# Hybrid decoder mixer on one Trainium2 core: projections in quarter chunks, and half of the conv group moved from beside the sample attention to beside the prompt attention

## The chip, the cores and the metric

One core of one Trainium2 chip runs the whole program as one launch. The metric is device time in microseconds (us). All tensors come and go as float32. An engine takes its own instructions in order from its own queue: TensorE (PE), VectorE (DVE), ScalarE (ACT), GpSimd (POOL) and SyncE (SP, which issues most DMAs). Every order named below is an order within one such queue.

## What is computed

One decoder layer on 1024 prompt rows and 32 sample rows (8 requests of 4 tokens): an FFN, the mixer, a second FFN, a final norm. Only the mixer is touched:

```python
p = rms_norm(x) @ w_in           # columns: q | k | v | forget logits | B gate | C gate | conv input
uc = cg * u                      # conv group: C gate times conv input
# head group A: 8 heads of 64, forgetting attention
s = q.k/8 + sum of log f between key and query      # causal
o_prompt = softmax(s) @ v                            # 1024 x 1024, blocks of 128 queries
o_sample = softmax over 2048 paged cache rows and 4 new rows, per request
# head group B: 512 channels, short conv of width 3 over time
y = conv_w[0]*uc[t-2] + conv_w[1]*uc[t-1] + conv_w[2]*uc[t];   conv_out = bg * y
x = x + concat(rms_norm(o), rms_norm(conv_out)) @ w_out
```

The cache of keys and the cache of values are each read once through a page table: 8 requests x 16 pages of 128 rows x 512 float32, 33.6 MB each.

## The kernel before, in words

**A projection** has 128 columns of w_in. `K.weight` (L91) loads them, 0.524 MB, in one DMA issued by SP (L75, three buffers), and splits each half into a float32r head `wh` (ACT, L86) and rest `wl` (DVE, L88). The 1056 rows of the normed x lie in SBUF as `XH` and `XL`. `win` (L612) makes one *window*: 352 rows, 8 row blocks of D, three matmuls each (L103 to L105, `wh` by `XH`, `wh` by `XL`, `wl` by `XH`), so 24 matmuls into one bank `pg`. A projection is three windows. q, k and v are four projections each, the conv group is four tiles of three projections (C gate, conv input, B gate) and nine windows a tile. A conv tile also reads its 8 KB state and writes an 8 KB state (`out_cso`, L929), in its own small pieces.

**The sample attention** (`sample(g)`, L813, g = two groups of four requests) is a generator. Its cache comes in 64 *chunks* of four pages (`fetch`, L772: two pages issued by SP after a page number is read, two gathered by POOL; four buffers, fetched up to four ahead), 1.05 MB each. Order: 16 key chunks of group 0, 16 value chunks of group 0, 16 key chunks of group 1, 16 value chunks of group 1. A key chunk is 16 short matmuls into `sc` (L832), a value chunk 16 calls into `pv` (L874), all with 32-wide column tiles. The values of a group also need the new values, so `sample(0)` waits for `vnew` (all v projections).

**The driver** (L972 to L982) walks through the k projections, the v projections and the four conv tiles, window by window, and after each window takes 1.2, 0.9 or 1.5 steps of the sample generator (`RK`, `RV`, `RC`); what remains runs at the end.

**The prompt attention** (L1112 to L1128) follows and has the PE to itself: 8 heads x 8 query blocks of 128. Per block: `logits` (L1041, matmuls with `KA`/`KB` into `S`, a mask), softmax on ACT and DVE, `flip` (L1062: transposes of P in groups of up to four into a bank `ptp`, two banks, copied out by ACT), and every second block `weigh` (L1077: P times V for two query blocks into `O`, two banks). Even heads hold P and V as float32r heads and rests and use two matmuls of 128 x 128 by up to 256 columns (L1089, L1090); the rest of P costs a DVE subtraction (L1075). Odd heads (`NATIVE`) keep float32 and use 64-wide weights (L1085), which run as two passes. Logits run three blocks ahead, `weigh` four behind. The norm of the conv output (`conv_norm`, L999) is put in after blocks 28 and 60. `load_qk` (L1026) loads a head's operands one head ahead; behind that of head 6 the loads of w_out are allowed to start (`K.after`).

A framework scheduler places the instructions of these generators on each engine's queue with the waits that the data and buffers need; the queues below are what it made.

Of the kernel before, what the change touches and what calls it, by code (L numbers as in the profile page):

```python
# [39 lines left out]
NATIVE = (1, 3, 5, 7)  # L40
LA, PVD, PTB, PRB = 3, 4, 3, 4
CONV_AT = (28, 60)
RK, RV, RC = 1.2, 0.9, 1.5
# [384 lines left out]
def kernel(ctx: ExitStack, tc: tile.TileContext, io: dict):  # L428
# [141 lines left out]
    with ExitStack() as es:  # L570
# [41 lines left out]
        def win(ws, c, m=P):  # L612
            ps = pg.tile([P, 512], F32, tag="pg", name="pg")[:m, :MC]
# [7 lines left out]
        def proj(i, kind, t):  # L621

            ws = K.weight(io["w_in"][i], D)
            for c in range(NMC):
                ps = win(ws, c)
# [130 lines left out]
        forget(lambda: next(qs[0]))  # L756
# [31 lines left out]
        new = []  # L788
# [24 lines left out]
        def sample(g):  # L813
# [25 lines left out]
            pn = ptr.tile([P, 512], F32, tag="tr", name="pn")[:, :NS]  # L839
            QN = smp.tile([P, NHP, 32], F32, tag="QN", bufs=1, name="QN")  # L840
# [10 lines left out]
            if g == 0:  # L851
                load_gates(1)
            yield
            PT = smp.tile([P, PAGES + 1, P], F32, tag="PT", bufs=1, name="PT")
# [8 lines left out]
            yield  # L863
            while not new:
                yield
# [17 lines left out]
            nc.scalar.activation(M, pv, AF.Copy, scale=sm)  # L883
# [19 lines left out]
        def conv():  # L903
            for t in range(4):
# [8 lines left out]
                for c in range(NMC):  # L913
                    ps = win(ws, c)
                    g_ = mix.tile([P, MC], F32, tag="cg", bufs=3, name="cg")
                    nc.scalar.copy(g_, ps)
                    cg.append(g_)
                    yield
                ws = K.weight(io["w_in"][20 + t], D)
                for c in range(NMC):  # L920
                    ps = win(ws, c)
# [24 lines left out]
                for c in range(NMC):  # L946
                    ps = win(ws, c)
# [5 lines left out]
        def values():  # L953
            for t in range(NHP):
                ws = K.weight(io["w_in"][8 + t], D)
                for c in range(NMC):
                    ps = win(ws, c)
# [25 lines left out]
    es_x.close()  # L983
# [5 lines left out]
    opc = pool(es_r, "op_c")  # L989
    xo = [None] * NCH  # L990
    with ExitStack() as es:
        ap_ = pool(es, "ap", "left")
        ptr = pool(es, "ptr2", space=PSUM)
# [16 lines left out]
        def load_v(hp):  # L1010
            vt = ap_.tile([P, SEQ], F32, tag="vt", bufs=1, name="vt")
            nc.sync.dma_start(vt, v_d[hp])
            V = ap_.tile([P, 8, 2, HD], F32R, tag="V", bufs=2, name="V")
            VF = ap_.tile([P, 8, HD], F32, tag="VF", bufs=2, name="VF")
            for j0 in range(0, 8, 4):
                pt_ = ptr.tile([P, 512], F32, tag="tr", bufs=2, name="ptv")
# [3 lines left out]
                pv_ = pt_.rearrange("p (j a d) -> p j a d", j=4, a=2)  # L1020
                nc.scalar.copy(V[:, j0:j0 + 4, 0, :], pv_[:, :, 0, :])
                nc.vector.tensor_sub(V[:, j0:j0 + 4, 1, :], pv_[:, :, 0, :], V[:, j0:j0 + 4, 0, :])
                nc.scalar.copy(VF[:, j0:j0 + 4, :], pv_[:, :, 1, :])
            return V, VF

        def load_qk(h):  # L1026
# [5 lines left out]
            for dst, src in ((KA[:HD], kh[pr, :]), (KA[HD:], kh[pr, :]),  # L1032
# [3 lines left out]
                ins = nc.sync.dma_start(dst.bitcast(F32), src)  # L1036
            if h == 6:
                K.after = ins.ins
# [23 lines left out]
        def flip(h, i, Pr, pt2):  # L1062

            c0 = P * (i % 2)
            for j0 in range(0, i + 1, 4):
                n = min(4, i + 1 - j0)
                pt_ = ptr.tile([P, 512], F32, tag="tr", bufs=2, name="ptp")
# [3 lines left out]
                pv_ = pt_[:, :n * P].rearrange("p (j q) -> p j q", q=P)  # L1071
                hi = pt2[0][:, j0:j0 + n, c0:c0 + P]
                nc.scalar.copy(hi, pv_)
                if h not in NATIVE:
                    nc.vector.tensor_sub(pt2[1][:, j0:j0 + n, c0:c0 + P], pv_, hi)  # L1075

        def weigh(h, m, pt2):  # L1077
            V, VF = vs[h // 2]
            pr = slice(HD * (h % 2), HD * (h % 2) + HD)
            O = ppv.tile([P, 512], F32, tag="pv", bufs=2, name="O")  # L1080
            nj = 2 * m + 2
            for j in range(nj):
                c0 = P if j == nj - 1 else 0
                if h in NATIVE:
                    nc.tensor.matmul(O[:HD, c0:256], VF[:, j, :], pt2[0][:, j, c0:], start=j == 0,  # L1085
                                     stop=j == nj - 1)
                else:
                    w = V[:, j].rearrange("p c d -> p (c d)")
                    nc.tensor.matmul(O[:, c0:256], w, pt2[0][:, j, c0:], start=j == 0, stop=False)  # L1089
                    nc.tensor.matmul(O[:, c0:256], w, pt2[1][:, j, c0:], start=False, stop=j == nj - 1)  # L1090
            at = ap_.tile([P, 256], F32, tag="at", bufs=3, name="at")
            if h in NATIVE:
                nc.scalar.copy(at[pr], O[:HD, :256])
            else:
                nc.scalar.copy(at[pr], O[HD:, :256])
                nc.vector.tensor_add(at[pr], O[:HD, :256], at[pr])
            nc.sync.dma_start(at_d[h // 2][pr, 256 * m:256 * m + 256], at[pr])
# [237 lines left out]
```

## Time and profile before

| | us |
|---|---|
| three runs | 2160.84, 2164.36, 2169.01 (median 2164.36) |
| profiled execution | 2163.56, span 2161.8 |
| FFN 1, norm, q projections, forget gate | 0 to 819.5 |
| k, v, conv projections beside the sample attention | 819.5 to 1143.5 |
| prompt attention | 1143.5 to 1308.4 |
| w_out and FFN 2 | 1308.4 to 2161.8 |

The stages are cut where the PE's lines change. 1.76 us of the time lie around the span. In the timeline, PE instructions overlap: the time that one costs is the distance to the start of the next, not its printed length.

### The profile page before, as it was taken

The numbers are of one execution on the slowest core, as the hardware profiler recorded it, in microseconds if no ns is written. First come the engines' busy times: TensorE is split into PE (matmuls) and PEld (weight loads), VectorE is DVE, ScalarE is ACT, GpSimd is POOL, SyncE is SP. The second block draws the span as 40 slices with busy tenths as digits, with TensorE's granted clock in tenths as the row PEclk, the third lists the DMA queues.
The fourth block names the chain that finished last, engine by engine and source line by source line (L and its number), as shares of the span: only waits on it lengthen the run. The fifth ranks groups of instructions, "written<-read, shape, count | busy, mean of one in ns | idle before, by whom it ended". The sixth has DMA issues, their size and how long they took to land. (4 is left out here: it accounts for less than half of the span.)

```text
span 2161.8 us, 42854 instructions
## 1 busy us (share of the span) xinstructions
PE 2098.5 (97%) x16738; PEld 1995.7 (92%) x16738; DVE 1352.4 (63%) x2604; ACT 876.1 (41%) x1754; POOL 264.3 (12%) x367
## 2 busy tenths in 40 slices
PE   7999999999999989999898999999999999999998
PEld 7999999999999877897697777999999999999997
DVE  8877777776656742322226785897677677775354
ACT  6533333344434422211115774453333333454343
POOL 0010001110000054234340000001010101100000
PEclk9999999999999989999998999999999999999999
DMA  6222222247546549869886436432222222496353
GB/s 212 77 93 91 84 85 93 93 162 238 198 139 212 167 150 329 297 201 312 253 262 142 111 95 201 144 107 88 76 80 73 86 85 84 142 311 210 108 180 131
DMA packets 138795, 335.15 MB, mean 155 GB/s; under 512 B 28144, under 2 KB 47568, under 8 KB 137056
## 3 DMA queue, kind: packets, MB, share of 16 engines
q1 hardware_dynamic: 116736, 263.66, 38.6%
q0 software_dynamic: 21856, 68.76, 9.1%
q8 instruction: 131, 2.15, 0.4%
q14 instruction: 72, 0.59, 0.1%
HBM read 276.09 MB, written 56.24 MB: 154 GB/s over the span
## 5 line engine op out<-in xcount | busy, mean ns | idle before, releaser
L103 PE MATMUL ps<-op,wh 128*128 128x264 f32 x2604 | 742.2, 285 | 2.9 <-ACT op L192 2.4
L105 PE MATMUL ps<-op,wl 128*128 128x264 f32 x2604 | 744.4, 286 | 0.0
L104 PE MATMUL ps<-op,wh 128*128 128x264 f32 x2604 | 743.1, 286 | 0.0
L86 ACT CAST wh<-wraw 128x512 fp32r<-128x512 f32 x536 | 312.8, 600 | 487.6 <-PE ps L104 281.3
L88 DVE TENSOR_TENSOR wl<-wraw,wh 128x512 fp32r<-128x512 f32 x536 | 347.3, 663 | 250.1 <-ACT wh L86 238.7
L103 PEld LDWEIGHTS ps<-op,wh 128*128 128x128 f32 x2604 | 492.8, 189 | 4.4 <-ACT op L192 2.8
L104 PEld LDWEIGHTS ps<-op,wh 128*128 128x128 f32 x2604 | 491.4, 189 | 0.4 <-DVE op L193 0.2
L105 PEld LDWEIGHTS ps<-op,wl 128*128 128x128 f32 x2604 | 491.5, 189 | 0.2
L103 PE MATMUL ps<-h,wh 128*128 128x264 f32 x1408 | 402.0, 285 | 0.0
L104 PE MATMUL ps<-h,wh 128*128 128x264 f32 x1408 | 400.5, 284 | 0.0
L105 PE MATMUL ps<-h,wl 128*128 128x264 f32 x1408 | 398.1, 283 | 0.5 <-DVE wl L88 0.5
L105 PEld LDWEIGHTS ps<-h,wl 128*128 128x128 f32 x1408 | 264.9, 188 | 0.7 <-DVE wl L88 0.7
L104 PEld LDWEIGHTS ps<-h,wh 128*128 128x128 f32 x1408 | 264.8, 188 | 0.2
L103 PEld LDWEIGHTS ps<-h,wh 128*128 128x128 f32 x1408 | 264.8, 188 | 0.2
L103 PE MATMUL pg<-XH,wh 128*128 128x352 f32 x576 | 196.0, 340 | 8.2 <-DVE zl L631 4.2
L104 PE MATMUL pg<-XL,wh 128*128 128x352 f32 x576 | 190.5, 331 | 0.0
L105 PE MATMUL pg<-XH,wl 128*128 128x352 f32 x576 | 189.7, 329 | 0.0
L86 ACT CAST wh<-s 128x512 fp32r<-128x512 f32 x176 | 107.7, 616 | 115.7 <-PE ps L104 106.9
L103 PEld LDWEIGHTS pg<-XH,wh 128*128 128x128 f32 x576 | 111.6, 194 | 34.7 <-issue 11.9
L88 DVE TENSOR_TENSOR wl<-s,wh 128x512 fp32r<-128x512 f32 x176 | 120.7, 690 | 26.6 <-ACT wh L86 22.5
L326 POOL DMA_DIRECT2D h_d<-t x79 | 42.7, 540 | 598.3 <-DVE t L325 598.3
L104 PEld LDWEIGHTS pg<-XL,wh 128*128 128x128 f32 x576 | 111.8, 194 | 0.0
(274 smaller groups left out, 2610.5 us busy)
## 6 DMA issues: line engine op xcount, KB each, us to landing
wraw<-in_w2a SPq DMA_DIRECT2D x48, 512.0 KB
wraw<-in_w2b SPq DMA_DIRECT2D x48, 512.0 KB
h_d<-t POOLq DMA_DIRECT2D x176, 132.0 KB, 2.0
h<-h_d SPq DMA_DIRECT2D x88, 264.0 KB
kvraw<-in_kc SPq DMA_DIRECT2D x64, 256.0 KB
kvraw<-in_vc SPq DMA_DIRECT2D x64, 256.0 KB
wraw<-in_w1a SPq DMA_DIRECT2D x28, 512.0 KB
wraw<-in_w3a SPq DMA_DIRECT2D x28, 512.0 KB
```

Source lines behind the costliest of these rows:

```text
L86: nc.scalar.copy(wh, x)
L88: nc.vector.tensor_sub(wl, x, wh)
L103: nc.tensor.matmul(ps, w[0], x[0], start=start, stop=False)
L104: nc.tensor.matmul(ps, w[0], x[1], start=False, stop=False)
L105: nc.tensor.matmul(ps, w[1], x[0], start=False, stop=stop)
L326: nc.gpsimd.dma_start(h_d[2 * p + 1][:, f, :], t)
```

## The change

- `win` becomes a generator that yields after every 6 of its 24 matmuls (a quarter). The rates become 0.34, 0.34 and 0.45 sample steps a quarter (1.36, 1.36, 1.8 a window).
- `sample(g)` is cut in `sample_keys(g)` and `sample_values(g)`; the cache is walked as keys 0, keys 1, values 0, values 1, so two `PT` (transposed probabilities) exist at once.
- `conv` takes a list of tiles: 0 and 1 stay beside the sample attention, 2 and 3 (18 windows) run beside the prompt attention, at 2.6 steps of the `prompt` generator a quarter. For this `XH`, `XL`, the buffers `mixb` and two `pg` banks live on; `ptp`/`ptv` and `O` go from two banks to one each.
- P times V: all heads keep float32 and one `V`. The two query blocks of a pair go to the two 64-row halves of `O` by 64-wide column tiles, alternating; 128 columns each, two passes each. The float32r rests, their subtractions and `NATIVE` go.
- `weigh` two blocks behind (was four), five P buffers (was three); both `conv_norm` after the last conv tile, among the last blocks; `K.after` is gone.

The core of the diff:

```diff
-RK, RV, RC = 1.2, 0.9, 1.5
+RK, RV, RC = 0.34, 0.34, 0.45
+CONV_A = 2
+RP = 2.6
...
-            K.dot(ps, ws, [(XH[:, k, cs], XL[:, k, cs]) for k in range(KD)])
+            for k in range(0, KD, 2):
+                K.dot(ps, ws[k:k + 2], [(XH[:, i, cs], XL[:, i, cs]) for i in (k, k + 1)], k == 0, k == KD - 2)
+                if k < KD - 2:
+                    yield
             return ps
...
         for g in range(2):
             chunks += [(io["kc"], 4 * g + b, j) for j in range(4) for b in range(4)]
+        for g in range(2):
             chunks += [(io["vc"], 4 * g + b, j) for b in range(4) for j in range(4)]
...
-        A = chain(sample(0), sample(1))
+        A = chain(sample_keys(0), sample_keys(1), sample_values(0), sample_values(1))
         due = 0.0
-        for work, rate in ((chain(*(proj(NHP + t, "k", t) for t in range(NHP))), RK),
-                           (values(), RV), (conv(), RC)):
+        for work, rate in ((k_proj(), RK), (values(), RV), (conv(range(CONV_A)), RC)):
...
+        mix = pool(es, "mixb", "left")
+        pg = es.enter_context(tc.tile_pool(name="pgb", bufs=2, space=PSUM, reuse_waits="tile"))
...
-                pt_ = ptr.tile([P, 512], F32, tag="tr", bufs=2, name="ptp")
+                pt_ = ptr.tile([P, 512], F32, tag="tr", bufs=1, name="ptp")
...
+            O = ppv.tile([P, 512], F32, tag="pv", bufs=1, name="O")[:, :P]
+            halves = [slice(0, HD), slice(HD, P)]
+            for j in range(2 * m + 2):
+                for b, (pr, pt) in enumerate(zip(halves, pt2)):
+                    n = 2 * m + b
+                    if j <= n:
+                        nc.tensor.matmul(O[pr], V[:, j, vc], pt[:, j, :], start=j == 0, stop=j == n)
+                if j == 3 and m > 1:
+                    yield
...
+        A = prompt()
+        due = 0.0
+        for _ in conv(range(CONV_A, 4)):
+            due += RP
+            while due >= 1:
+                next(A, None)
+                due -= 1
```

POOL's queue from the forget-gate gathers (`R`) to the last cache gather, as a difference; one gather is one page, `in_kc` keys, `in_vc` values:

```order
 L599 DMA R<-in_lf,idl 128x128 x5
+L599 DMA kvraw<-in_kc,idx 128x512 x32
+L825 MEMSET S 128x96
 L599 DMA kvraw<-in_kc,idx 128x512 x24
-L599 DMA kvraw<-in_vc,idx 128x512 x8
-L818 MEMSET S 128x96
-L599 DMA kvraw<-in_vc,idx 128x512 x24
-L599 DMA kvraw<-in_kc,idx 128x512 x32
-L599 DMA kvraw<-in_vc,idx 128x512 x32
```

The alternation of keys and values by groups is gone: all 64 key gathers come first, and the 64 value gathers follow as one run.

PE's queue at the last value chunks of the sample attention; before:

```order
L105 MATMUL pg<-XH,wl 128x352
L874 MATMUL pv<-kvraw,PT 32x128 x32
L879 MATMUL pv<-VS,PT 32x128 x4
L103 MATMUL pg<-XH,wh 128x352
L104 MATMUL pg<-XL,wh 128x352
L105 MATMUL pg<-XH,wl 128x352
```

and after:

```order
L105 MATMUL pg<-XH,wl 128x352
L887 MATMUL pv<-kvraw,PT 32x128 x32
L892 MATMUL pv<-VS,PT 32x128 x4
L887 MATMUL pv<-kvraw,PT 32x128 x64
L892 MATMUL pv<-VS,PT 32x128 x4
L103 MATMUL pg<-XH,wh 128x352
L104 MATMUL pg<-XL,wh 128x352
L105 MATMUL pg<-XH,wl 128x352
```

Before, a whole window of projection follows the last chunks; now six chunks stand in a row, without a projection between them.

PE's queue in the middle of the prompt attention, at an even head; before:

```order
L1089 MATMUL O<-PTh,V 128x256
L1090 MATMUL O<-PTl,V 128x256
L1049 MATMUL S<-KA,QA 128x512
L1050 MATMUL S<-KB,QB 128x512
L1069 MATMUL ptp<-cst,Pr 128x128 x4
L1052 LDWEIGHTS idb
L1052 MATMUL S<-diag,idb 128x128
L1049 MATMUL S<-KA,QA 128x512
L1050 MATMUL S<-KB,QB 128x512
```

and after, where the conv tiles 2 and 3 run:

```order
L1079 MATMUL ptp<-cst,Pr 128x128 x4
L103 MATMUL pg<-XH,wh 128x352
L104 MATMUL pg<-XL,wh 128x352
L105 MATMUL pg<-XH,wl 128x352
L103 MATMUL pg<-XH,wh 128x352
L104 MATMUL pg<-XL,wh 128x352
L1079 MATMUL ptp<-cst,Pr 128x128
L105 MATMUL pg<-XH,wl 128x352
L1060 MATMUL S<-KA,QA 128x128
L1061 MATMUL S<-KB,QB 128x128
```

Projection matmuls now stand between one group of transposes and the next, and between transposes and logits.

## Rows read from the trace of the kernel before

**Rows 1.** Page, part 1: busy us, share of span, instructions.

```profile
PE 2098.5 (97%) x16738; PEld 1995.7 (92%) x16738; DVE 1352.4 (63%) x2604; ACT 876.1 (41%) x1754; POOL 264.3 (12%) x367
```

**Rows 2.** Windows by stage: stretch, length, then the columns named.

```profile
core 0: us, PE busy (x) PEld busy (x) DVE busy (x) ACT busy (x) POOL busy (x), PEclk, DMA share, GB/s
...
819.50:889.60 70.10, 67.91 (x421) 51.82 (x421) 16.16 (x31) 18.24 (x40) 29.92 (x32) 0.98 1.00 348
889.60:938.60 49.00, 48.84 (x317) 46.44 (x316) 14.22 (x22) 14.41 (x27) 3.30 (x4) 1.00 0.56 196
938.60:1006.00 67.40, 64.67 (x825) 58.62 (x828) 12.55 (x26) 10.12 (x19) 30.28 (x32) 0.97 0.85 284
1006.00:1071.00 65.00, 56.99 (x360) 42.58 (x356) 14.69 (x33) 6.93 (x13) 28.75 (x30) 0.92 0.91 274
1071.00:1143.50 72.50, 72.50 (x893) 67.29 (x886) 19.92 (x41) 13.72 (x25) 26.93 (x29) 1.00 0.79 233
1143.50:1165.00 21.50, 16.24 (x71) 12.94 (x70) 11.22 (x32) 7.69 (x23) 3.20 (x6) 0.68 0.67 163
1165.00:1308.40 143.40, 139.65 (x866) 103.40 (x864) 114.17 (x254) 108.99 (x265) 0.00 (x0) 1.00 0.42 101
```

**Rows 3.** Timeline of PE, 828.9 to 834.5: start, length, line, operation, count.

```profile
828.96 0.32 PE L104 MATMUL pg<-XL,wh 128*128 128x352 f32 x1
829.12 0.32 PE L105 MATMUL pg<-XH,wl 128*128 128x352 f32 x1
829.37 1.07 PE L832 MATMUL sc<-kvraw,QZ 128*32 128x512 f32 x8
830.37 0.43 PE L103 MATMUL pg<-XH,wh 128*128 128x352 f32 x1
...
834.43 0.64 PE L832 MATMUL sc<-kvraw,QZ 128*32 128x512 f32 x4
```

**Rows 4.** Windows: the fastest long stretch, and one behind a state write.

```profile
840.00:900.00 60.00, 60.00 (x395) 47.49 (x388) 18.04 (x30) 13.91 (x29) 25.61 (x26) 1.00 1.01 366
1025.00:1032.00 7.00, 7.00 (x48) 5.34 (x48) 0.98 (x3) 0.00 (x0) 3.21 (x5) 1.00 0.84 43
```

**Rows 5.** DMA view, 1022 to 1034: packets, and one of its issues.

```profile
DMA packets 1898, 1.82 MB, mean 152 GB/s; under 512 B 1295, under 2 KB 1295, under 8 KB 1897
...
out_cso<-E SPq DMA_DIRECT2D x1, 8.0 KB
```

**Rows 6.** Timeline of PE, 1036 to 1052: a key chunk that waits.

```profile
1046.90 1.93 PE L832 MATMUL sc<-kvraw,QZ 128*32 128x512 f32 x8 [8.01 <-DMA kvraw<-in_kc]
```

**Rows 7.** Timeline of PE, 1097.6 to 1100: a value chunk.

```profile
1097.92 1.08 PE L874 MATMUL pv<-kvraw,PT 128*32 128x128 f32 x32
```

**Rows 8.** Timeline of PE, 1150 to 1160: the first transposes of V.

```profile
1156.76 1.97 PE L1018 MATMUL ptv<-cst,vt 128*128 128x128 f32 x8 [2.12 <-DMA vt<-v_d]
```

**Rows 9.** Timeline of PE, 1301.8 to 1308.6: last P times V, odd head.

```profile
1301.94 6.48 PE L1085 MATMUL O<-PTh,VF 128*64 128x256 f32 x32
```

**Rows 10.** Groups by form in 1301.8 to 1308.6: the shapes of these 32.

```profile
L1085 PE MATMUL O<-PTh,VF 128*64 128x256 f32 x26 | 6.2, 381 | 0.0
L1085 PE MATMUL O<-PTh,VF 128*64 128x128 f32 x6 | 1.1, 272 | 0.0
```

**Rows 11.** Groups by form, PE, 1143.5 to 1310: all odd heads.

```profile
L1085 PE MATMUL O<-PTh,VF 128*64 128x256 f32 x128 | 33.6, 389 | 0.3 <-ACT rs L169 0.3
...
L1085 PE MATMUL O<-PTh,VF 128*64 128x128 f32 x32 | 6.4, 282 | 0.0
```

**Rows 12.** Timeline of PE, 1255.9 to 1256.5: even heads.

```profile
1256.11 0.28 PE L1090 MATMUL O<-PTl,V 128*128 128x256 f32 x1
1256.23 0.28 PE L1089 MATMUL O<-PTh,V 128*128 128x256 f32 x1
```

**Rows 13.** Timeline of all engines, 1299.8 to 1302.9: transposes, then their copies.

```profile
1300.91 1.09 PE L1069 MATMUL ptp<-cst,Pr 128*128 128x128 f32 x8
1301.61 1.07 ACT L1073 COPY PTh<-ptp 128x512 f32<-128x512 f32 x2 [0.38 <-PE ptp L1069]
```

More of the change, by code (lines that the diff above doesn't have):

```diff
@@ L624, in proj @@
             for c in range(NMC):
-                ps = win(ws, c)
+                ps = yield from win(ws, c)
                 cs, n = cols(c)
@@ L755 @@
         qs = [proj(t, "q", t) for t in range(NHP)]
-        forget(lambda: next(qs[0]))
+        forget(lambda: [next(qs[0]) for _ in range(4)])
         for g in qs:
@@ L787 @@
         taken = []
-        new = []
+        keys, new = [], []
         def kv_chunk():
@@ L839, in sample @@
             pn = ptr.tile([P, 512], F32, tag="tr", name="pn")[:, :NS]
+            if g == 0:
+                load_gates(1)
+            while not keys:
+                yield
             QN = smp.tile([P, NHP, 32], F32, tag="QN", bufs=1, name="QN")
@@ L901, in vnew, with conv @@
             new.append(VS)
-        def conv():
-            for t in range(4):
+        def conv(ts):
+            for t in ts:
                 q = nc.gpsimd if t == 3 else nc.sync
@@ L913, in conv @@
                 for c in range(NMC):
-                    ps = win(ws, c)
+                    ps = yield from win(ws, c)
                     g_ = mix.tile([P, MC], F32, tag="cg", bufs=3, name="cg")
@@ L920, in conv @@
                 for c in range(NMC):
-                    ps = win(ws, c)
+                    ps = yield from win(ws, c)
                     cs, n = cols(c)
@@ L946, in conv @@
                 for c in range(NMC):
-                    ps = win(ws, c)
+                    ps = yield from win(ws, c)
                     st = mix.tile([P, MC], F32, tag="st", bufs=3, name="st")
@@ L956, in values @@
                 for c in range(NMC):
-                    ps = win(ws, c)
+                    ps = yield from win(ws, c)
                     cs, n = cols(c)
@@ L970, in chain, with k_proj @@
                 yield from g_
[L972 removed]
+        def k_proj():
+            for t in range(NHP):
+                yield from proj(NHP + t, "k", t)
+            keys.append(True)
+        A = chain(sample_keys(0), sample_keys(1), sample_values(0), sample_values(1))
         due = 0.0
[L974 to L975 removed]
+        for work, rate in ((k_proj(), RK), (values(), RV), (conv(range(CONV_A)), RC)):
             for _ in work:
@@ L982 @@
             pass
-    es_x.close()
     for t in range(NHP):
@@ L1099 @@
         qk, vs, prs, pts = {}, {}, {}, {}
-        blocks = [(h, 2 * m + j) for h in range(H) for m in range(4) for j in range(2)]
-        qk[0] = load_qk(0)
+        blocks = [(h, i) for h in range(H) for i in range(8)]
         def ahead(n):
@@ L1126, with behind, prompt @@
-        for k in range(len(blocks) - PVD, len(blocks)):
-            if k % 2:
-                weigh(blocks[k][0], blocks[k][1] // 2, pts.pop((blocks[k][0], blocks[k][1] // 2)))
+        def behind(k):
+            if k >= 0 and k % 2:
+                h, i = blocks[k]
+                yield from weigh(h, i // 2, [pts.pop(k - 1), pts.pop(k)])
+        def prompt():
+            qk[0] = load_qk(0)
+            for n in range(LA):
+                ahead(n)
+                yield
+            for n, (h, i) in enumerate(blocks):
+                ahead(n + LA)
+                yield
+                pts[n] = ap_.tile([P, 8, P], F32, tag="PT", bufs=PTB, name="PT")
+                yield from flip(i, prs.pop(n), pts[n])
+                yield from behind(n - PVD)
+            for k in range(len(blocks) - PVD, len(blocks)):
+                yield from behind(k)
@@ new lines @@
+        A = prompt()
[5 more added lines that the diff above has]
+                due -= 1
+        es_x.close()
+        opc = pool(es_r, "op_c")
+        rest = list(range(NCH // 2))
+        for n, _ in enumerate(A):
+            if n % 8 == 7 and rest:
+                c = rest.pop(0)
+                conv_norm(c, ap_.tile([P, 4, CH], F32, tag="co", bufs=1, name="co"),
+                          pg.tile([P, 512], F32, tag="pg", name="pco")[:, :CH])
@@ L1131 @@
+        for c in rest:
+            conv_norm(c, ap_.tile([P, 4, CH], F32, tag="co", bufs=1, name="co"),
+                      pg.tile([P, 512], F32, tag="pg", name="pco")[:, :CH])
     es_ps = ctx.enter_context(ExitStack())
```

89 lines of the change are left out of this document (26 added, 63 removed).

## The prediction

> **What bounds the kernel now.** I read the page's shares first. PE is busy for 97% of the span [rows 1], so a gain must come from PE work that disappears, from PE work that gets cheaper, or from the few stretches in which PE waits or has the low clock. To find these I read the windows by stage [rows 2], PE's idle being the length less its busy time. Beside the sample attention (819.5 to 1143.5, 324.0 us) it idles 13.1 us, 8.0 of them in one key chunk that waits for its load [rows 6]; the clock column adds some 9 us, most of it in the stretch with that wait (0.92). At the start of the prompt attention (1143.5 to 1165) it idles 5.3 us and the granted clock is 0.68 of 2.4 GHz, that is, partly the 1.2 GHz level: 0.32 x 21.5 = 6.9 us, together 12.2 us lost in 21.5. In the rest of the prompt attention it idles 3.7 us of 143.4. So the only places to win in are the sample stage, that start, and the form of P times V.
>
> DMA is the second resource. Rate times length in the five sample rows gives 24.4 + 9.6 + 19.1 + 17.8 + 16.9 = 87.8 MB, a mean of 271 GB/s. Its share is 0.79 to 1.00 in four of the five [rows 2]; the fifth, 889.6 to 938.6 (0.56), is where the value chunks of group 0 wait for the new values while projections run alone. The rate at full share is 366 GB/s over 60 us, but 43 GB/s for 7 us at a share of 0.84 [rows 4]: there 1295 of 1898 packets are under 512 B, behind the state write of a conv tile [rows 5]. The key chunk that waits 8.01 us comes right after [rows 6].
>
> **The prices.** A projection matmul starts every 0.16 us; from projection to key chunk it is 0.25, so the change of tile width costs 0.09, and about 0.1 on the way back; a key chunk takes 1.00 us, a window with both changes 834.43 - 830.37 = 4.06, thus 3.86 alone [rows 3]. A value chunk is 1.0 too [rows 7]. The last 32 passes of an odd head take 6.48 us [rows 9] and are 26 of 256 columns and 6 of 128 [rows 10]: 6.48 / 29 = 0.223 us a pass of 256, 0.112 a pass of 128. On even heads one of 256 starts every 0.12 us [rows 12].
>
> **Sample stage: -10 us.** 17 of the 18 moved windows lie in these 324.0 us (the last one follows the last chunk, as PE's order shows), so the work that stays takes 324.0 - 17 x 3.86 = 258.4 today. After the change PE needs 42 windows x 3.86 = 162, 64 chunks x 1.0 = 64 and some 5 for the rest: 231. DMA has 87.8 less six weights (3.1 MB) and two tiles' outputs (1.1 MB), 83.6 MB; at 366 GB/s that is 228, and two state writes of 7 us with almost no rate make 242. So DMA is the bound now: a k window with 1.36 chunks takes 5.2 us of PE and carries 1.43 MB of cache, 0.17 of weight and 0.53 of outputs, 2.13 MB, 410 GB/s, above what the rows reach. The hole at 889.6 goes, because keys of group 1 need no new values; that is what the new cache order buys. I take 340 GB/s over the stage: 246, and 2 for the six chunks at the end with no projection to hide their loads: 248, against 258.4. The ends are 240 (-18: the 366 with the state writes mostly hidden) and 290 (+32: see the second rival). SP issues half the pages, the weights and the outputs in one queue, so a page that waits for one of four buffers holds the next weight back; three weight buffers cover that, and where not, PE waits for `wh`. POOL's gathers only change names and order.
>
> **Moved windows.** Their 69.5 us of PE reappear beside the prompt attention. They bring 3.1 MB there, where DMA has 0.42 share [rows 2]; the two state writes meet loads that are issued a head (some 20 us) early: 0. ACT and DVE are busy 109.0 and 114.2 of 143.4 us [rows 2] and get the splits of six weights and 18 evacuations in a stage that grows by some 60: 0. If that cover goes, PE waits for its softmax, as in the 3.7 us of today.
>
> **Start of the prompt attention: -11 us.** The first logits, softmax and transposes of V wait for loads and for each other [rows 8]. Some 170 projection matmuls (27 us) now stand among them, so PE neither idles nor loses its clock: 12.2 less 1 that I leave. In the steady part the waits shrink by 3.
>
> **P times V: -13.7 us.** Today: 128 passes of 256 and 32 of 128 on odd heads [rows 11], 128 x 0.223 + 32 x 0.112 = 32.1; on even heads 64 + 64 matmuls of 256 and 32 of 128, 15.4 + 1.9 = 17.3; sum 49.4. After: 36 calls a head, 20 slots if the two halves run side by side, 20 x 2 passes x 0.112 x 8 heads = 35.7. If they run one after the other, 36 x 2 x 0.112 x 8 = 64.5 (+15.1). No row has two 64-wide tiles at once. The nearest is the value chunk: 32 passes of 128 columns in four 32-wide tiles in 1.0 us [rows 7]; one after the other they would be 32 x 0.112 = 3.6, so nearly four ran at once. I take side by side.
>
> The Trainium skill, "TensorEngine Tiling (Array Packing)", Tiling Modes, lists 128x64 as two independent tiles, up to 2 times. By it the term would be the 35.7 too; no run shown here has that mode.
>
> **Changes of width: +6.3 us.** PE's order has 63 runs of `O` instead of 30, since projections and transposes cut them; 33 x 0.19.
>
> **Single banks: +12 us.** Eight transposes start at 1300.91, the first copy at 1301.61, and two copies take 1.07 [rows 13]. So a four-transpose bank is held 0.70 + 0.54 = 1.24 us, 0.43 of it transposing: the next flip needs 0.81 us of other PE work ahead, five projection matmuls. Of the 96 flips most have that (the third place in PE's order has just five between a group of four and the next); I charge 15 in full. Ends: 0, and 36 x 0.81 = 29.
>
> **Tail: +3 us.** Both norms of the conv output now come among the last blocks, one of them was at block 28. The nearest row is the 2.12 us wait [rows 8]: between 0 and twice that.
>
> **Sum.** -10 - 11 - 3 - 13.7 + 6.3 + 12 + 3 = -16.4 against the profiled 2163.6, which is 0.8 below the median: 2147.
>
> **The rivals.**
>
> *All covers hold* (2124): the sample stage takes 240 and neither banks nor tail cost: 16.4 + 8 + 12 + 3 = 39 off. For it: 60 us at 366 GB/s [rows 4]. Against: the state writes remain.
>
> *Transfers hold their present rate* (2189, slower): the mix of gathers, outputs and weights gives no more than the 274 to 284 GB/s of two of the rows [rows 2], though there at a share of 0.85 to 0.91; at 290 the stage takes 83.6 / 290 = 288 + 2, 32 longer than 258.4 instead of 10 shorter, and the sum is +25. The whole gain is gone from 318 GB/s down (stage 265), and it is 0.5% slower from 306 down. For it: half the cache comes by gathers, and a k window has three outputs. Against: 348 and 366 were reached in just this mix, k outputs included.
>
> The Trainium skill, "Perfetto Trace Analysis", DMA Optimizations, says that DMAs under 2 KB have a significant overhead per transfer; it gives no rate for these, and the 43 GB/s above agree. It speaks for this rival, since outputs and state writes stay beside the cache, and for its 2189.
>
> *The halves run one after the other* (2176): +28.8 on P times V. For it: no row has the pair. Against: the four tiles of the value chunk.
>
> *The fill doesn't fill* (2158): the projections stand in the queue, but wait for their own weights behind the operands of the first heads in SP's queue, so the start costs what it does now: +11.
>
> **How the numbers follow.** 0.5% is 11 us, about what a measurement of this kernel can tell from no change; the bounds are 2153 and 2175. Forecast 0.55, own range 2130 to 2162 (0.42 faster, 0.13 same). All covers 0.12 (faster). Transfers 0.18 (0.12 slower, 0.06 same, since it is a scale of rates). One after the other 0.10 (half and half). No fill 0.05 (0.04 same, 0.01 faster). Faster 0.55, same 0.28, slower 0.17. The range goes from 2114 to 2184: below lies the best end of the covers, above the slower half of the transfers.
>
> **What would show it.** In the profile after: the sample stage some 248 us with a DMA rate near 340 and a share near 1.0 (at 290 the second rival); no window at a clock of 0.68 at the start of the prompt attention; `O` passes of a pair 0.11 us a slot and pass (0.22: one after the other); idle before `ptp` with ACT's copy as releaser, near 12 us. Wrong altogether it would be if PE waited for `wh` or for P in the long stage, or if the clock fell in the sample stage because PE now waits for pages in many small pieces.

## The result, and the profile after

The changed kernel took 2180.7 us (median of 7, 2174.8 to 2184.8) against 2164.3 (median of 7): a ratio of 1.0074, 95% interval 1.0055 to 1.0093. It is slower, by 16 us, where 17 us less were forecast. 2180.7 lies inside the stated range (2114 to 2184), on the other side of no change. That it lies inside is luck: the upper part of the range stood there for slow transfers, and the cause was another.

PE is as busy as before [rows 1]:

```profile
PE 2103.6 (97%) x16994; PEld 1988.2 (91%) x16994; DVE 1338.3 (61%) x2564; ACT 874.3 (40%) x1744; POOL 264.4 (12%) x367
```

The share tells nothing; the stages do. I cut both traces at the same events: the first k window, the end of the sample attention (before: the last projection window; after: the last value chunk), and the first matmul of w_out. Windows of the kernel before over these stretches (columns as in [rows 2]):

```profile
815.60:1146.40 330.80, 317.71 (x2846) 273.39 (x2845) 78.61 (x158) 63.42 (x124) 124.16 (x133) 0.97 0.84 270
1146.40:1308.30 161.90, 152.89 (x916) 113.39 (x914) 124.32 (x278) 116.68 (x287) 1.21 (x3) 0.96 0.44 109
```

and of the kernel after, from the first k window, first the v part, the conv part and its end, then the start, the long part and the end of the prompt attention, and the first piece of w_out:

```profile
817.60:891.30 73.70, 68.76 (x417) 50.10 (x416) 14.91 (x29) 17.34 (x39) 33.16 (x35) 0.95 0.98 337
891.30:956.60 65.30, 64.97 (x425) 50.03 (x421) 16.39 (x26) 14.21 (x27) 26.77 (x28) 1.00 0.98 334
956.60:1053.50 96.90, 93.96 (x1129) 79.77 (x1127) 22.05 (x45) 17.71 (x32) 45.45 (x48) 0.98 0.87 300
1053.50:1090.60 37.10, 28.46 (x450) 22.40 (x448) 5.46 (x13) 2.63 (x5) 14.56 (x16) 0.87 0.93 278
1090.60:1115.00 24.40, 24.40 (x143) 23.20 (x140) 8.19 (x26) 6.10 (x15) 2.22 (x4) 0.91 0.69 156
1115.00:1300.00 185.00, 181.99 (x1370) 146.03 (x1369) 106.95 (x242) 107.44 (x265) 3.08 (x5) 1.00 0.39 95
1300.00:1317.60 17.60, 14.22 (x99) 9.58 (x97) 7.19 (x12) 9.79 (x20) 0.00 (x0) 0.81 0.17 47
1317.60:1350.00 32.40, 24.36 (x133) 21.01 (x132) 18.02 (x26) 12.86 (x24) 0.00 (x0) 0.84 0.61 189
```

If the 18 moved windows are taken out of both stages at the forecast's price of 69.5 us, the 17.1 us between the two spans divide so:

| stage | before | after | change | forecast |
|---|---|---|---|---|
| up to the first k window | 815.6 | 817.6 | +2.0 | 0 |
| sample stage | 330.8 - 69.5 = 261.3 | 273.0 | +11.7 | -10 |
| prompt attention | 161.9 | 227.0 - 69.5 = 157.5 | -4.4 | -9.4 (start, waits in the steady part, P times V, widths, banks) |
| from w_out on | 853.5 | 861.3 | +7.8 | +3 |

In the sample stage PE idles 16.8 us (13.1 before), and the clock (0.96 over the stage, 0.97 before) costs up to 10.9 (9.9 before), less where the low clock falls into idle time. What PE waited for in the sample stage (waits of PE, 817.6 to 1090.6; us, times, longest):

```profile
PE pv L887 <- DMA kvraw<-in_vc: 8.9, 7, 4.3
PE sc L839 <- ACT QZ L641: 4.9, 1, 4.9
PE pv L887 <- DMA kvraw<-in_vc,idx: 2.7, 3, 1.4
```

The 8.01 us wait for a key chunk [rows 6] is gone, and the start of the prompt attention, 5.3 us idle at a clock of 0.68 before [rows 2], has no idle time at 0.91. Both as forecast. In their place stand waits for value pages, most of them in the last stretch (0.87 clock, 8.6 us idle in 37.1), and a wait of 4.9 us for q at the first key chunk (2.2 before).

But waits are only one part; PE's own need is larger than forecast. Without idle time and the low clock, the stage takes PE 273.0 - 16.8 - 10.9 = 245.3 us, or somewhat more, since some of the low clock is idle time and is taken off twice: e14_mendbs (below), at a clock of 1.00 and with hardly a wait, has 248.5. The forecast had 231. The timeline of PE at a value chunk shows why:

```profile
1037.71 1.08 PE L887 MATMUL pv<-kvraw,PT 128*32 128x128 f32 x32
1038.72 0.43 PE L103 MATMUL pg<-XH,wh 128*128 128x352 f32 x1
1038.98 0.33 PE L104 MATMUL pg<-XL,wh 128*128 128x352 f32 x1
1039.14 0.32 PE L105 MATMUL pg<-XH,wl 128*128 128x352 f32 x1
```

The chunk is 1.01 to the next start, and the first projection behind it takes 0.26 instead of 0.16; with 0.09 ahead of the chunk [rows 3] a chunk that stands alone costs 1.2. I had read these two changes in the rows, taken them out of the window (4.06 to 3.86), and not put them on the chunk: 64 x 0.2 = 13 us, most of the difference of 14 to 17. DMA has its slow stretches behind the two state writes as before [rows 4] (windows, kernel after); the waits between 1071 and 1090 follow the first of these two:

```profile
1058.00:1064.00 6.00, 6.00 (x95) 5.16 (x94) 0.53 (x1) 0.00 (x0) 2.93 (x4) 1.00 0.75 56
997.00:1003.00 6.00, 6.00 (x96) 5.16 (x94) 0.58 (x2) 0.00 (x0) 3.62 (x4) 1.00 0.63 88
```

The same cost of cutting is there beside the prompt attention, where I priced the moved windows at 69.5 us flat. The timeline there:

```profile
1126.06 0.32 PE L105 MATMUL pg<-XH,wl 128*128 128x352 f32 x1
1126.26 0.33 PE L1079 MATMUL ptp<-cst,Pr 128*128 128x128 f32 x1
1126.35 0.41 PE L103 MATMUL pg<-XH,wh 128*128 128x352 f32 x1
1126.59 0.32 PE L104 MATMUL pg<-XL,wh 128*128 128x352 f32 x1
1126.75 0.32 PE L105 MATMUL pg<-XH,wl 128*128 128x352 f32 x1
```

Behind the first projection matmul after a single transpose, the next one starts 0.24 us later instead of 0.16. The 432 projection matmuls there take 81.5 us from start to next start, 12 more than 69.5; some 2 of these are the low clock of the first stretch (0.91 over 24.4 us), the rest falls on 78 pieces. P times V, taken in the same way, went from 63.6 to 52.1. Pairs do run side by side (timeline, kernel after): 30 passes of 128 columns in 1293.26 - 1291.36 = 1.90 us, 0.063 each; one after the other they would take 30 x 0.112 = 3.4.

```profile
1291.36 1.97 PE L1093 MATMUL O<-PT,V 128*64 128x128 f32 x30
...
1293.26 0.50 PE L1060 MATMUL S<-KA,QA 128*128 128x512 f32 x1
```

The forecast charged 33 more cuts into `O`, 63 runs instead of 30. In the trace of the kernel before `O` already stands in 64 runs, 63 after; one call of `weigh` there is cut like this (timeline, kernel before):

```profile
1192.35 0.65 PE L1085 MATMUL O<-PTh,VF 128*64 128x256 f32 x2
1192.92 0.44 PE L1069 MATMUL ptp<-cst,Pr 128*128 128x128 f32 x2
1193.29 2.16 PE L1085 MATMUL O<-PTh,VF 128*64 128x256 f32 x10
```

What the change cuts anew are the transposes (71 runs before, 95 after) and the projections.

### The profile page after: what moved, and what is told of

It is laid out like the page before. It is cut to its first block, busy times and chain, and to the rows that moved or that the text cites. A ratio compares the mean times of both kernels' runs of the same rounds, so it can differ in the third digit from the quotient of the medians.

```text
span 2178.9 us, 43341 instructions
## 1 busy us (share of the span) xinstructions
PE 2103.6 (97%) x16994; PEld 1988.2 (91%) x16994; DVE 1338.3 (61%) x2564; ACT 874.3 (40%) x1744; POOL 264.4 (12%) x367
## 4 chain that ended last, share of the span: by engine, by line
PE 87%; DMA 6%; DVE 2%; ACT 2%; SPq 1%; issue 1%; POOL 1%; DVEq 0%; ACTq 0%; POOLq 0%
PE ps L104 22%; PE ps L105 22%; PE ps L103 22%; PE pg L103 4%; PE pg L104 3%; PE pg L105 3%; PE O L1093 2%; PE ptp L1079 2%; PE sc L839 2%; DMA kvraw<-in_vc 1%; PE ps L142 1%; PE S L1060 1%; PE pv L887 1%; DMA wraw<-in_w_out 1%; PE S L1061 1%
## 5 line engine op out<-in xcount | busy, mean ns | idle before, releaser
L103 PE MATMUL pg<-XH,wh 128*128 128x352 f32 x576 | 200.7, 348 | 9.3 <-ACT QZ L641 5.9
L105 PE MATMUL pg<-XH,wl 128*128 128x352 f32 x576 | 190.8, 331 | 0.0
```

Of the source, the lines that this page charges most:

```text
L103: nc.tensor.matmul(ps, w[0], x[0], start=start, stop=False)
L105: nc.tensor.matmul(ps, w[1], x[0], start=False, stop=stop)
```

## Experiments: the sample stage

Stage lengths below run from the first k window to the last value chunk (273.0 in the changed kernel), or to the last projection where all conv tiles are beside the sample attention. The runs e5_cso2 to e8_all4b2 belong to a series in which the kernel before took 2185.9 us, mostly because the part ahead of this stage was longer; there I compare ratios, or stages of runs of that series. Each stage length is that of one profile. The stage of the changed kernel, with nothing in it changed, took 273.0, 272.1 (e2_cso), 269.9 (e11_banks) and 265.7 us (e7_rp22), so a difference of a few us between series shows nothing.

**Rate.** One number:

```diff
-RK, RV, RC = 0.34, 0.34, 0.45
+RK, RV, RC = 0.34, 0.34, 0.54
```

> The changed kernel with one number changed: 0.54 sample steps a quarter (was 0.45) while the conv tiles 0 and 1 are projected, so that no value chunk is left when they end. In the changed kernel the stage from the first k window to the last value chunk took 273.1 us; the last six chunks stand in a row from 1071 to 1090 and lose some 15 us to waits for their pages and to the low clock. Theory (the rate was too low; the loss is that of chunks without projections beside them): the stage falls to about 261, the whole by 8 to 14 us. Rival (the conv phase is bound by DMA, 41 MB and two slow state writes, whatever the order): the waits only move among the windows, the stage stays within 4 us of 273, the whole within 4 us.

Measured: 2173.8 us, ratio 1.0053 (1.0032 to 1.0073), stage 268.0. It lies between the two expectations: 5 us of the stage. Waits for value pages still sum to 9.4 us: the chunks without projections beside them were only a part of it.

**State writes, first try.** The writes of tiles 0 and 1 were put at a later place in the code:

```diff
-                q.dma_start(io["cso"][t], E_[:, :, NT:])
+                if t < 2:
+                    late.append((io["cso"][t], E_[:, :, NT:]))
+                else:
+                    q.dma_start(io["cso"][t], E_[:, :, NT:])
```

> The changed kernel with the state writes of conv tiles 0 and 1 issued later, beside the prompt attention, where DMA has room; nothing else. Theory (each write holds DMA for some 7 us at under 80 GB/s, empties the four page buffers, and both stalls of value chunks, at 1009 and at 1071, come right behind one): the waits of PE for value pages fall from 11.6 us to under 4, the stage from 273.1 to about 264, the whole by 6 to 11 us. Rival (the waits at the end come from six chunks in a row, not from the write): the wait at 1009 goes (3 us), that at the end stays, the whole falls by under 4 us.

Measured: 2177.3, ratio 1.0063 (1.0042 to 1.0084), stage 272.1. It tested nothing: the scheduler issued the two writes at 994 and 1065 us, still among the value chunks (993 and 1055 in the changed kernel). A place in the code is not a place in the queue.

**State writes, held.** The same, with an order edge behind the loads of head 2 (`issue_after`: the write stands behind that load in the queue):

```diff
+                with tc.issue_after(held[nq // 20 - 1]):
+                    nc.sync.dma_start(*late.pop(0))
```

> The changed kernel with the state writes of conv tiles 0 and 1 held back behind the loads of the prompt attention's head 2 (in the earlier try the scheduler had put them back among the value chunks, at 994 and 1065 us, so that it tested nothing). Theory (the writes empty the page buffers): waits for value pages, 11.6 us in the changed kernel, fall under 4, the stage from the first k window to the last value chunk from 273.0 to about 262. Rival (the six chunks in a row at the end are what waits, since they need 6.3 MB in 7 us of PE time): the wait at 1009 goes, that at the end stays at 6 us or more, the stage is about 268.

Measured: ratio 1.0062 (1.0041 to 1.0084). The writes now went out at 1117 and 1135, and the stage took 259.9. In this series the same rates with the writes in place (e7_rp22, below, which differs only behind this stage) took 265.7, so the writes are worth 6 us of the stage. Windows of the stage, e5_cso2:

```profile
845.40:1105.30 259.90, 253.35 (x2400) 200.47 (x2402) 59.15 (x112) 51.87 (x101) 114.04 (x121) 0.98 0.94 328
```

and e7_rp22:

```profile
842.40:1108.10 265.70, 253.32 (x2403) 199.57 (x2406) 59.09 (x112) 51.80 (x101) 113.53 (x121) 0.99 0.93 319
```

The idle time is 6.6 against 12.4 with the same PE work: the theory holds in the waits, the rate went from 319 to 328 GB/s. Yet the whole hardly gained (1.0062 against 1.0074): the prompt attention took 230.1 us here (227.0 in the changed kernel). Whether the moved writes did that is not shown.

**Whole windows.** The quarter chunks undone in this stage alone:

```diff
-                if k < KD - 2:
+                if k < KD - 2 and not coarse[0]:
                     yield
```

> The changed kernel with whole windows (24 matmuls) between steps of the sample attention, at four times the rate each, so the same steps a window; quarters stay beside the prompt attention. It undoes the quarter chunks in the sample stage alone. Theory (every chunk that stands alone between projections costs 0.2 us of changes of width, some 64 of them where whole windows would make about 45 groups): PE's own need falls by about 4 us, the stage from 273.1 to about 269. Rival (quarters are what lets pages arrive in time): with two chunks in a row waits for pages appear and the stage is 5 to 15 us longer.

Measured: 2181.3, ratio 1.0086 (1.0065 to 1.0107), stage 270.0. Both were right in part: PE idles 17.3 us (16.8) at a clock of 0.95 (0.96), so its own need fell by some 6 us, and half of that was lost again, most of it to the lower clock. The whole time did not move: measured on it, quarters are worth nothing here, and cost nothing.

**All four conv tiles beside the sample attention.** The move undone, all else kept:

```diff
-RK, RV, RC = 0.34, 0.34, 0.45
-CONV_A = 2
+RK, RV, RC = 0.34, 0.34, 0.27
+CONV_A = 4
```

> The changed kernel with all four conv tiles beside the sample attention again (0.27 steps a quarter, so that the chunks last to the end) and the prompt attention by itself: the move undone, quarters, cache order, P times V and single banks kept. Before, these two stages took 492.8 us together, changed 500.0. Theory (the move costs more than it gains: 78 entries of the projection stream beside the prompt attention at 0.15, 12 us, the late conv norm 8 us, and the lack of projections at the end of the sample stage 15 us, against 12 us of the fill at the start): sample stage 322, prompt attention 155 to 165, w_out some 6 earlier, the whole 10 to 20 us faster than the changed kernel. Rival (the move gains its fill, and single banks alone are worse without projections between): prompt attention over 175, the whole equal to the changed kernel or slower.

Measured: 2190.7, ratio 1.0124 (1.0094 to 1.0155), slower than the changed kernel. The sample stage took 324.8 as expected (322) and w_out on 852.6, but the prompt attention 190.8. So the rival won: what is moved covers something there. What, the next section shows. In the sample stage no wait for a page is left; the one long wait is that for q (waits, e4_all4):

```profile
PE sc L839 <- ACT QZ L641: 5.3, 1, 5.3
```

## Experiments: the prompt attention

PE's waits in e4_all4's prompt attention:

```profile
PE ptp L1079 <- ACT PT L1081: 12.0, 20, 2.6
PE S L1060 <- DMA QA<-q_d: 10.5, 1, 10.5
```

**Two transpose banks** with all four tiles beside the sample attention:

```diff
-        pg = es.enter_context(tc.tile_pool(name="pgb", bufs=2, space=PSUM, reuse_waits="tile"))
+        pg = es.enter_context(tc.tile_pool(name="pgb", bufs=1, space=PSUM, reuse_waits="tile"))
...
-                pt_ = ptr.tile([P, 512], F32, tag="tr", bufs=1, name="ptp")
+                pt_ = ptr.tile([P, 512], F32, tag="tr", bufs=2, name="ptp")
```

> All four conv tiles beside the sample attention, as in the earlier run of that, and two banks for the transposes again (one for the norm sums; O keeps one). That run's prompt attention took 190.8 us against 162.0 before, though P times V got 11 us cheaper. Theory (the single transpose bank is what made it slow: the move of conv tiles takes banks, and only projections between hide that): prompt attention 152 to 165, the whole 2150 to 2165, as before or faster. Rival (the single O bank, the blocks' shorter lead or late loads made it slow): prompt attention over 175, the whole over 2175.

Measured: ratio 1.0019 (1.0006 to 1.0032), against 1.0124 with one bank; prompt attention 174.1 instead of 190.8, and the wait for transposes 3.0 instead of 12.0:

```profile
PE S L1060 <- DMA QA<-q_d: 10.5, 1, 10.5
...
PE ptp L1079 <- ACT PT L1081: 3.0, 7, 0.6
```

Between the two expected ranges in the prompt attention: the bank is worth 17 us, and a wait of 10.5 us for q stays. The sample stage of this run is the one to note. It has all 60 windows and no wait over 1.0 us (windows, e8_all4b2):

```profile
843.80:1161.70 317.90, 316.93 (x2845) 266.99 (x2844) 78.67 (x153) 64.57 (x125) 116.65 (x125) 1.00 0.83 274
```

So the new order of chunks with 60 windows as cover does away with the stage's waits, although all state writes stand in it; with 42 windows, in the changed kernel, it does not.

**P times V alone**, put into the kernel before (banks and schedule kept):

```diff
-                if h in NATIVE:
-                    nc.tensor.matmul(O[:HD, c0:256], VF[:, j, :], pt2[0][:, j, c0:], start=j == 0,
-                                     stop=j == nj - 1)
...
+                for b, pr in enumerate(halves):
+                    n = 2 * m + b
+                    if j <= n:
+                        nc.tensor.matmul(O[pr], V[:, j, vc], pt2[0][:, j, P * b:P * b + P], start=j == 0, stop=j == n)
```

> The kernel before with the new P times V alone: float32 for all heads, the two query blocks of a pair in the two 64-row halves of O by alternating 64-wide column tiles, no float32r rests; two banks each for transposes and O stay, and all of the schedule. P times V took 63.6 us of PE before (starts to next starts) and 52.1 changed. Theory (the new form is worth 11 us by itself, since pairs run side by side, and the waits on the rest of P go with it): prompt attention from 162.0 to 145 to 151, the whole 10 to 16 us faster than before, about 2151. Rival (with the short matmuls PE waits for softmax or copies instead): prompt attention 155 or more, the whole within 6 us of before.

Measured: ratio 1.0026 (1.0014 to 1.0039), prompt attention 166.0. It looked like the rival, but the wait was not for softmax: it was the wait for q again. SP's timeline in e6_pv:

```profile
1142.97 12.72 SPq L781 DMA_DIRECT2D kvraw<-in_vc  x8
1174.63 0.81 SPq L1154 DMA_DIRECT2D x<-x_d  x2
1175.53 1.16 SPq L1032 DMA_DIRECT2D KA<-k_d  x2
```

SP issues nothing from 1155.7 to 1174.63, just after the last projection matmul has started (1174.28): the x loads of the w_out stage stand first in its queue, they take the place of XH and must wait for its last reader, and head 0's loads wait behind them. In the kernel before the scheduler had the same loads in the other order, with `KA` at 1127.

**The same with the x loads held** behind head 0's first load:

```diff
-                nc.sync.dma_start(xs[c][i], x_d[c][:, 4 * i:4 * i + 4, :])
+                with tc.issue_after(first[0]):
+                    nc.sync.dma_start(xs[c][i], x_d[c][:, 4 * i:4 * i + 4, :])
```

> The kernel before with the new P times V alone, as in the earlier run of that, and the two x loads of the w_out stage held behind the loads of head 0's q and k. In that earlier run SP's queue had the x loads, which wait until the last projection has read XH, ahead of head 0's loads, and PE waited 12 us for q at the start of the prompt attention (before: 5 us of small waits there). Theory (P times V is worth 11 us, and the earlier run lost them again to that place in SP's queue): wait for q under 2 us, prompt attention from 166.0 to 148 to 154, the whole 0.4 to 0.8% faster than before. Rival (head 0's loads are late for their buffers' sake, not for the x loads): the wait stays near 10 us, the whole within 0.3% of before or slower.

Measured: 2156.4, ratio 0.9969 (0.9956 to 0.9982), faster than before; prompt attention 153.6, no wait for q. In SP's queue:

```profile
1118.43 12.90 SPq L781 DMA_DIRECT2D kvraw<-in_vc  x8
1131.42 1.16 SPq L1034 DMA_DIRECT2D KA<-k_d  x2
```

The gain is at the low end: the prompt attention's 8 us, of which the whole kept 7. `O` itself fell from 63.6 to 48.4 us, from start to next start, while the transposes rose from 34.1 to 39.7; why they did is not shown. So the new P times V is worth some 8 us here, and a wait elsewhere can hide all of it.

**The same edge in e8_all4b2:**

> Quarter chunks, new cache order and new P times V, all four conv tiles beside the sample attention, two transpose banks, as in the earlier run of that, with the x loads held in the same way. That run had a sample stage of 317.9 us without a wait of over 1.3 us, a prompt attention of 174.1 with 12 us of waits for q, and a ratio of 1.0019. Theory: the wait for q goes, with it the low clock behind it; prompt attention 156 to 162, the ratio 0.992 to 0.997, faster than before. Rival (single O bank or transposes are what is left): prompt attention still over 170, ratio over 1.000.

Measured: 2157.2, ratio 0.9969 (0.9958 to 0.9980), prompt attention 161.2. The theory holds on its edge; 5.6 us of waits on the single O bank are left there. Without any moved window the change's other parts, with two transpose banks and the order edge, give 7 us; that is no more than P times V with the edge gave alone (e9_pvx, also 0.9969).

**Banks the other way round in the changed kernel** (the diff of e8_all4b2 alone):

> The changed kernel (conv tiles 2 and 3 moved) with the banks of the prompt attention dealt out otherwise: two for transposes, one for the projections that run beside it. Theory (projections hide the single transpose bank nearly wholly in the changed kernel: transposes cost 36.7 us there against 34.1 before, and 5.5 us of idle waits for copies): two banks win 3 to 6 us there; the single projection bank costs 18 evacuations of about 0.5 us, unless other work stands between: 0 to 9 us; the whole within 6 us of the changed kernel. Rival (single transpose bank is a large part of the loss): 10 us or more faster.

Measured: 2166.9, ratio 1.0017 (1.0008 to 1.0026), 14 us faster than the changed kernel: the rival. The prompt attention went from 227.0 to 218.5, from w_out on 861.3 to 857.4; the other 3 us lie in the sample stage (269.9), which the edit doesn't touch. The idle time before transposes says little of it (5.5 us before, 3.1 after). With one bank PE's order has 63 runs of `O` and 95 of transposes, with two banks 43 and 70; from start to next start `O` fell from 52.1 to 47.4 us, transposes from 36.7 to 33.1.

**Steps beside the moved tiles**, so that they end earlier:

```diff
-RP = 2.6
+RP = 2.2
```

> The changed kernel with 2.2 prompt steps a quarter (was 2.6), so that conv tiles 2 and 3 end some 53 steps before the end of the prompt attention instead of 24, and both norms of the conv output come earlier. Theory (the late norm costs the 8 us that w_out and FFN 2 took longer, 861.3 against 853.5): from w_out on 853 to 855. At the same time 29 more steps run with single banks and no projections between, at some 0.25 us each by the unmoved version (190.8 us against 162.0 less 11.5, 40 us on 211 steps less its 11 us wait at the start): prompt attention 4 to 8 us longer, the whole within 4 us of the changed kernel. Rival (w_out's own loads are late because nothing holds them in order any more): from w_out on still 860 or more.

Measured: ratio 1.0061 (1.0037 to 1.0085); from w_out on 853.9, prompt attention 231.1 (227.0). Both as the theory says: the late norm is what w_out waited for, and of the 7.4 us won there 4.1 are paid back by more steps without cover. The longest of PE's waits from 1317.6 to 1350 in the changed kernel is for the normed conv output (waits; us, times, longest):

```profile
PE ps L103 <- ACT opc L192: 3.8, 1, 3.8
```

## Experiments: the parts put together

**Three repairs of the changed kernel**, the diffs of e1_rc54, e5_cso2 and e7_rp22 together:

> The changed kernel with three repairs at once: 0.54 sample steps a quarter beside conv tiles 0 and 1, the state writes of tiles 0 and 1 held back behind head 2's loads, and 2.2 prompt steps a quarter. Theory (what the runs so far gave one by one: about 5 us by the rate, 6 by the state writes, 8 at w_out less 4 in the prompt attention): 12 to 15 us faster than the changed kernel, ratio to before 0.998 to 1.002; the sample stage 255 to 258, just above PE's own need of 245 and the start wait. Rival (the moved form has another bound, DMA at 330 GB/s): sample stage over 262, ratio over 1.004.

Measured: 2156.5, ratio 0.9967 (0.9955 to 0.9979), 24 us faster than the changed kernel. The stage took 256.4, prompt attention 228.9, from w_out on 853.4. That is more than the 12 to 15 us expected. The surplus lies in the stage: 16.6 us shorter than in the changed kernel, 13.5 shorter than in e11_banks, which has the unrepaired stage in the same series; the parts came to 11. Windows of the stage, e12_mend:

```profile
818.60:1075.00 256.40, 250.16 (x2392) 197.65 (x2394) 57.36 (x109) 51.21 (x100) 119.23 (x126) 0.99 0.94 332
```

**With two transpose banks as well** (e13_mendb), **and with the sample attention started one step later** (e14_mendbs):

```diff
-        due = 0.0
+        due = -1.0
```

> The three repairs of the earlier run (0.54 steps a quarter, state writes held, 2.2 prompt steps a quarter; 2156.5 us, ratio 0.9967) and two transpose banks with one projection bank, which alone took the prompt attention from 227.7 to 218.5 us. Theory (the losses are separate): prompt attention from 228.9 to 218 to 222, ratio 0.991 to 0.995. Rival (they overlap: with 2.2 steps a quarter the bank's waits are in the part behind the conv tiles, and the single projection bank now costs as much): prompt attention over 225, ratio over 0.996.

> The same as e13_mendb with the sample attention started one step (three quarters of a window) later. In the changed kernel PE waits 4.9 us for q at the first key chunk, since only 18 projection matmuls stand between the last q window and it (before: 24, and 2.2 us). Theory (nine or so more quarters' matmuls, 3 us of work, cover it): the wait falls under 2 us, the stage is 2 to 4 us shorter than in e13_mendb. Rival (the wait only moves, since one more chunk is left for the end): the stage within 1.5 us of that of e13_mendb.

e13_mendb: 2157.6, ratio 0.9978 (0.9966 to 0.9990), prompt attention 226.8. The rival: on top of the other repairs the bank gives 2 us, not 9. The two overlap, and PE now waits 7.2 us for one softmax. e14_mendbs: 2150.5, ratio 0.9952 (0.9934 to 0.9970), the lowest of all, though its interval touches those of e9_pvx, e10_all4x, e12_mend and e13_mendb; its stage took 252.9 (257.5 in e13_mendb), the wait for q at the first chunk is gone, as expected. Windows of its stage:

```profile
820.60:1073.50 252.90, 248.53 (x2399) 197.57 (x2401) 59.36 (x111) 51.84 (x101) 120.11 (x126) 1.00 0.95 337
```

Now PE idles only 4.4 us in the stage, and is still busy for 248.5. That is the floor that the forecast put at 231; the 42 windows of projection alone take 177.3 us, from start to next start, where it had 162. The gain over e13_mendb is larger than this stage's 4.6 us; 4.3 more lie in the prompt attention (222.5), which no run takes apart.

## Why the prediction was wrong

- **Sample stage, -10, was +11.7.** Two steps failed. First, PE's need: the forecast put it at 231 us, below the 246 of the transfers, and so took DMA for the bound. It is 245 to 249, since a chunk alone between projections costs 1.2 and not 1.0, and quarter chunks leave nearly all of them alone; e14_mendbs, with hardly a wait, is still at 248.5. So PE is the floor, and the stage could not fall to 248 with any wait at all. Second, the covers: I took the waits to go with the new cache order. They do go where 60 windows stand beside it (e4_all4, e8_all4b2), but the move took 18 of these away at the same time. Slow state writes (6 us; the forecast had them as transfer time, not as waits), six chunks in a row (5 us by the rate) and the first chunk's wait for q (4.9 us, 2.2 before) came in. The rate of 315 GB/s lies just under the 318 at which the rival on transfers decides, but the mix as such was not the cause: with later writes and a higher rate of steps nearly the same bytes came at 332 and 337. What holds of that rival are the state writes. By the Trainium skill's "Perfetto Trace Analysis", DMA Optimizations, DMAs under 2 KB have a significant overhead per transfer; the stretch at 56 GB/s agrees, and taking two such writes out was worth 6 us.
- **Start of the prompt attention, -11: right in the main**, no idle time left there, while the clock of 0.91 still costs 2.2 us; and for a reason that I had not seen in full. The fill also covers head 0's loads, which in three runs without the move (e4_all4, e6_pv, e8_all4b2) came some 12 us late, until an order edge held the x loads back (e9_pvx, e10_all4x).
- **P times V, -13.7 and +6.3 for widths: the first right, the second not.** Pairs run side by side; together -11.5 where -7.4 was forecast. The +6.3 rests on 30 runs of `O` before, and the trace has 64: no cut came in there. Both ends were priced without these cuts or with part of them, 49.4 and 42.0 us against 63.6 and 52.1 measured, so that the difference came out nearer than either end is luck. By the Trainium skill's "TensorEngine Tiling (Array Packing)", Tiling Modes, two 128x64 tiles are independent; the 0.063 us a pass agrees.
- **Moved windows, priced at 69.5: 81.5.** The same slip as in the sample stage: every cut into the projections costs some 0.13 us (10 us on 78 pieces). I priced changes of width at `O`, where none came in, and not those of the projections. These 12 us alone are more than the 9.4 that I forecast as the gain of the prompt attention; P times V and the banks' idle time, both better than forecast, left 4.4 of it.
- **Single banks, +12, and waits in the steady part, -3: right in size, by chance.** The banks were priced as idle time, and only 5.5 us of that came; idle time behind the start went from 3.7 to 6.4 us. Dealing the banks out the other way is worth 8.5 us there, and goes with fewer cuts and not with less idle time (PE idles 10.2 us in it, 6.4 in the changed kernel), and with a clock of 0.99 instead of 0.98; that the cuts are the cause is argued from the counts, not shown by a run of its own. Without the projections one bank costs 17.
- **Tail, +3: 7.8**, beyond the twice 2.12 that I gave as its end: the late norm (e7_rp22).

The 2 us ahead of the first k window need not be an effect of the change: in e9_pvx, where nothing ahead of it is changed, the first key chunk starts 4.3 us later than in the kernel before (823.84, 819.55). What stays open is why e14_mendbs gains beside the prompt attention, and why the transposes of e9_pvx take longer.

## What to carry to other kernels

Price a finer interleave per piece: what it costs to enter and to leave a piece, times the number of pieces, on both kinds of work, before counting the waits that it hides. Count the pieces before and after in the same way. Work that is moved is also cover that is moved: ask at the place it leaves what waited unseen behind it. And when an edit shows no gain, look at which load stands first in the in-order queue at the next stage's start; here one order edge was worth the whole gain of a better inner loop.

## What the runs showed of the hardware

Behind an 8 KB state write in small pieces DMA moved 43 to 88 GB/s at a share of 0.63 to 0.84 for 6 to 7 us ([rows 4] and the two stretches of the kernel after). Two alternating 64-wide tiles took 0.063 us a pass of 128 columns, against 0.112 for one alone. The first projection matmul after a group of another kind holds its follower up by 0.08 to 0.10 us: 0.26 instead of 0.16 us behind a value chunk, 0.24 behind a single 128-wide transpose, so it is not the tile width alone.
